# Rotary embedding on one core: the rotated half summed by VectorE instead of TensorE, tables loaded over 128 partitions

## The chip, the cores and the metric

The kernel runs on one core of a Trainium2 chip. Its time is device microseconds (us) of that core, from start to end of the program. A core has TensorE (PE in the profile; matmuls, which write to PSUM), VectorE (DVE), ScalarE (ACT), GpSimd (POOL) and SyncE (SP), and 16 DMA engines that move data between HBM and SBUF. [...] SP, ACT and POOL can start DMAs.

## The reference

```
x: (16, 512, 1024) float32 -> (16, 512, 16 heads, 64)
cos, sin: (512, 32) float32, one row for each position
x1, x2 = x[..., :32], x[..., 32:]
out[..., :32] = x1 * cos - x2 * sin
out[..., 32:] = x1 * sin + x2 * cos
```

33.55 MB are read and 33.55 MB written. The two tables are 64 KB each.

## The kernel before

The 16 batches are taken two at a time: 8 slabs of 4 MB. A slab is a tile of 128 partitions x 8192 float32; a partition holds 8 consecutive rows (positions) of 1024 elements, so partitions 0 to 63 hold one batch and 64 to 127 the other. Five slab buffers exist (`slots = 5`). Results are written back into the slab that the input came in, so a buffer is free for the next load only when its store has landed.

At the start SP issues the first five loads (L69-70). ACT's queue issues the loads of `cos` and `sin` (L77), each over 64 partitions with 1 KB rows. POOL builds an identity `ident` and a two-fold copy of it, `spread`. VectorE turns the tables into bf16 rows `cc1` (cos, cos) and `ss1` (sin, -sin); TensorE copies them to all 128 partitions with `spread` (L104), and VectorE writes them out as `cc` and `ss` (L106).

Then each slab is worked off in 4 passes of 2 rows (2048 elements in a partition):

1. ScalarE casts the piece to bf16: `xb` (L115).
2. VectorE makes two products, `t1 = xb * cc` (L120) and `t2 = xb * ss` (L121), all bf16.
3. TensorE adds them in PSUM: for each 512-wide bank a matmul of `ident` with `t1` (L125) and one of `ident` with `t2` read with its 32-wide halves exchanged (L127), 8 matmuls in a pass.
4. ScalarE copies the sum from PSUM back into the slab as float32 (L132).

After the fourth pass ACT's queue issues the slab's store (L133), and SP issues the load of slab s+5 (L135, L66), which waits for that store to land. A framework orders each engine's instructions and puts in the semaphores. In the order that it made, ScalarE's cast of the next slab's first piece stands ahead of the write-backs of the last pieces of the slab before; a cast that waits for its load therefore holds up the write-backs and the store behind it. Intermediate tiles have 3 buffers each, the PSUM sum has 2.

Of the kernel before, what the change touches and what calls it, by code (L numbers as in the profile page):

```python
# [2 lines left out]

# [4 lines left out]


@with_exitstack  # L10
def kernel(
    ctx: ExitStack,
    tc: tile.TileContext,
    x: bass.AP,
    cos: bass.AP,
    sin: bass.AP,
    num_heads: int,
    out: bass.AP,
):
    nc = tc.nc  # L20
    P = nc.NUM_PARTITIONS

    batch, seq, dim = x.shape
    nh = num_heads
    hd = dim // nh
    half = hd // 2
    bf16 = mybir.dt.bfloat16
    f32 = mybir.dt.float32

    nb = 2  # L30
    slots = 5
    lead = 5
    nslabs = batch // nb
    rpp = nb * seq // P
    W = rpp * dim
    SP = seq // rpp
    rows = 2
    PW = rows * dim
    BANK = 512
    hpb = BANK // hd  # L40

    out_flat = out.rearrange("b s h d -> b s (h d)")

    singles = ctx.enter_context(tc.tile_pool(name="singles", bufs=1))
    slabs = ctx.enter_context(tc.tile_pool(name="slabs", bufs=slots))
    tpool = ctx.enter_context(tc.tile_pool(name="tpool", bufs=3))
    psum = ctx.enter_context(tc.tile_pool(
        name="psum", bufs=2, space=bass.MemoryType.PSUM))


    def dram(t, s):
        return bass.AP(tensor=t.tensor, offset=t.offset + s * nb * seq * dim,
                       ap=[[W, P], [1, W]])


    def view(t, offset, *dims):
        return dataclasses.replace(t, offset=t.offset + offset,
                                   ap=[t.ap[0], *[list(d) for d in dims]])


    slab = {}


    def load(s):
        slab[s] = slabs.tile([P, W], f32, tag="slab", name="slab")
        nc.sync.dma_start(out=slab[s], in_=dram(x, s))  # L66


    for s in range(lead):  # L69
        load(s)  # L70

    cos_sb = singles.tile([SP, rpp * half], f32, tag="cos_sb")
    sin_sb = singles.tile([SP, rpp * half], f32, tag="sin_sb")
    for t, src in ((cos_sb, cos), (sin_sb, sin)):
        nc.scalar.dma_start(out=t, in_=bass.AP(  # L77
            tensor=src.tensor, offset=src.offset,
            ap=[[rpp * half, SP], [1, rpp * half]]))

    ident = singles.tile([P, P], bf16, tag="ident")
    masks.make_identity(nc, ident)
    spread = singles.tile([SP, P], bf16, tag="spread")
    for g in range(P // SP):
        nc.gpsimd.tensor_copy(out=spread[:, g * SP:(g + 1) * SP],  # L85
                              in_=ident[:SP, :SP])


    cc1 = singles.tile([SP, rpp * hd], bf16, tag="cc1")
    ss1 = singles.tile([SP, rpp * hd], bf16, tag="ss1")  # L90
    nc.vector.tensor_copy(  # L91
        out=cc1, in_=view(cos_sb, 0, (half, rpp), (0, 2), (1, half)))
    sin_rows = view(sin_sb, 0, (half, rpp), (1, half))
    nc.vector.tensor_copy(  # L94
        out=view(ss1, 0, (hd, rpp), (1, half)), in_=sin_rows)
    nc.vector.tensor_scalar_mul(  # L96
        out=view(ss1, half, (hd, rpp), (1, half)), in0=sin_rows, scalar1=-1.0)
    cc = singles.tile([P, rpp * hd], bf16, tag="cc")
    ss = singles.tile([P, rpp * hd], bf16, tag="ss")
    for wide, one in ((cc, cc1), (ss, ss1)):  # L100
        acc = psum.tile([P, PW], f32, tag="acc", name="acc")
        for q in range(0, rpp * hd, BANK):
            n = min(BANK, rpp * hd - q)
            nc.tensor.matmul(view(acc, q, (1, n)), spread, view(one, q, (1, n)),  # L104
                             start=True, stop=True)
        nc.vector.tensor_copy(out=wide, in_=view(acc, 0, (1, rpp * hd)))  # L106

    for s in range(nslabs):
        xs = slab.pop(s)
        for k in range(rpp // rows):  # L110
            xk = view(xs, k * PW, (1, PW))
            xb = tpool.tile([P, PW], bf16, tag="xb")
            t1 = tpool.tile([P, PW], bf16, tag="t1")
            t2 = tpool.tile([P, PW], bf16, tag="t2")
            nc.scalar.copy(out=xb, in_=xk)  # L115

            def tab(t):
                return view(t, k * rows * hd, (hd, rows), (0, nh), (1, hd))

            nc.vector.tensor_mul(out=t1, in0=xb, in1=tab(cc))  # L120
            nc.vector.tensor_mul(out=t2, in0=xb, in1=tab(ss))  # L121
            acc = psum.tile([P, PW], f32, tag="acc")
            for q in range(0, PW, BANK):
                bank = view(acc, q, (1, BANK))
                nc.tensor.matmul(bank, ident, view(t1, q, (1, BANK)),  # L125
                                 start=True, stop=False)
                nc.tensor.matmul(  # L127
                    bank, ident,
                    view(t2, q + half, (hd, hpb), (-half, 2), (1, half)),
                    start=False, stop=True)  # L130

            nc.scalar.copy(out=xk, in_=acc)  # L132
        nc.scalar.dma_start(out=dram(out_flat, s), in_=xs)  # L133
        if s + lead < nslabs:
            load(s + lead)  # L135


# [1 line left out]
_INS = ['x', 'cos', 'sin', 'num_heads']  # L139
_OUTS = [((16, 512, 16, 64), 'float32')]  # L140

_NUMBERS = {'num_heads': 16}


# [26 lines left out]
```

## Time and profile before

| | |
|---|---|
| time, median of 7 runs | 163.75 us (163.36 to 165.43) |
| time of the profiled execution | 163.58 us |
| its span in the profile | 161.8 us |
| busy: TensorE, VectorE, ScalarE | 78.2, 76.4, 117.3 us |
| granted TensorE clock, mean | 0.845 |

Every DMA of a slab, from the trace (issue time, plus time from issue to landing; us from the start of the span):

| slab | load issued | load landed | store issued | store landed |
|---|---|---|---|---|
| 0 | 0.7 | 13.7 | 34.7 | 57.6 |
| 1 | 1.2 | 23.7 | 53.8 | 78.1 |
| 2 | 1.6 | 33.4 | 68.6 | 97.5 |
| 3 | 2.1 | 48.0 | 84.1 | 116.8 |
| 4 | 2.8 | 68.5 | 98.8 | 131.5 |
| 5 | 57.7 | 87.8 | 114.5 | 141.1 |
| 6 | 78.2 | 107.2 | 134.4 | 150.9 |
| 7 | 97.5 | 126.7 | 149.7 | 160.8 |

The loads run on SP's queue and the stores on ACT's. "Landed" is when the semaphore of the transfer was complete. Where transfers of both queues are in flight, they share the same 16 DMA engines.

### The profile page before, as it was taken

The page shows a single profiled execution, that of the slowest core. Times are in us where ns is not written, and L with a number is a line of the kernel's source. Part 1 is how long each engine was busy: PE and PEld are TensorE (multiplying, and loading weights), DVE is VectorE, ACT ScalarE, POOL GpSimd, SP SyncE. Part 2 cuts the span into 40 slices and gives each one's busy share as a digit, 9 for nine tenths or more (in the row PEclk, how much of TensorE's full clock was granted, in tenths as well). Part 3 has the DMA queues.
Part 4 walks back from the last instruction along what each step waited for, and adds up shares of the span by engine and source line. Part 5 has one row for each costly group of instructions (what it writes and reads, how often), then busy time and mean ns, then how long its engine had stood idle before and what let it go on. Part 6 is the DMA issues. An engine that isn't in the chain of part 4 may idle for free.

```text
span 161.8 us, 811 instructions
## 1 busy us (share of the span) xinstructions
PE 78.2 (48%) x253; PEld 28.8 (18%) x258; DVE 76.4 (47%) x69; ACT 117.3 (72%) x65; POOL 1.1 (1%) x8
## 2 busy tenths in 40 slices
PE   0001179636059754942995388079754078084000
PEld 0000024212013221310332133023221022021000
DVE  0001699055099439806955484199335172280000
ACT  3006746994999999899989998979990697918000
POOL 2000000000000000000000000000000000000000
PEclk9999999999857998696599968957999957659855
DMA  7999999999999999999999999999999999996996
GB/s 243 413 397 405 405 478 413 405 478 413 397 478 421 397 494 401 405 486 405 407 478 405 415 470 413 413 470 413 421 470 401 421 470 405 421 470 300 389 389 259
DMA packets 2468, 67.29 MB, mean 416 GB/s; under 512 B 288, under 2 KB 416, under 8 KB 416
## 3 DMA queue, kind: packets, MB, share of 16 engines
q1 hardware_dynamic: 1152, 33.55, 48.8%
q10 hardware_dynamic: 1312, 33.69, 48.4%
q8 instruction: 2, 0.03, 0.1%
q14 instruction: 2, 0.02, 0.0%
HBM read 33.69 MB, written 33.55 MB: 416 GB/s over the span
## 4 chain that ended last, share of the span: by engine, by line
DMA 46%; PE 16%; ACT 14%; issue 9%; DVE 6%; ACTq 0%; DVEq 0%; SPq 0%
DMA slab<-in_x_dram 18%; DMA out_dram<-slab 18%; DMA sin_sb<-in_sin_dram 10%; PE acc L127 9%; ACT slab L132 8%; PE acc L125 7%; ACT xb L115 6%; DVE t L121 5%; DVE t L120 1%; PE acc L104 0%; ACTq L77 0%; DVE ss L94 0%; DVE ss L96 0%; DVEq L120 0%; ACTq L132 0%
## 5 line engine op out<-in xcount | busy, mean ns | idle before, releaser
L125 PE MATMUL acc<-t,ident 128*128 128x512 bf16 x123 | 56.4, 459 | 43.9 <-DVE t L120 33.3
L115 ACT CAST xb<-slab 128x2048 bf16<-128x2048 f32 x32 | 59.6, 1905 | 19.3 <-DMA slab<-in_x_dram 16.7
L132 ACT COPY slab<-acc 128x2048 f32<-128x2048 f32 x32 | 59.2, 1869 | 11.1 <-PE acc L127 10.6
L120 DVE TENSOR_TENSOR t<-xb,cc 128x2048 bf16<-128x2048 bf16 x32 | 39.1, 1222 | 51.4 <-ACT xb L115 51.4
L127 PE MATMUL acc<-t,ident 128*128 128x512 bf16 x128 | 57.6, 450 | 7.9 <-DVE t L121 7.3
L121 DVE TENSOR_TENSOR t<-xb,ss 128x2048 bf16<-128x2048 bf16 x32 | 39.0, 1218 | 0.0
L127 PEld LDWEIGHTS <-ident 128*128 128x128 bf16 x128 | 14.4, 112 | 58.6 <-issue 50.3
L125 PEld LDWEIGHTS <-ident 128*128 128x128 bf16 x128 | 14.2, 111 | 47.1 <-issue 28.7
L104 PE MATMUL acc<-cc,spread 64*128 64x512 bf16 x1 | 0.6, 582 | 12.8 <-DVE cc L91 12.8
L91 DVE CAST cc<-cos_sb 64x512 bf16<-64x512 f32 x1 | 0.4, 418 | 12.3 <-DMA cos_sb<-in_cos_dram 12.3
L104 PE MATMUL acc<-ss,spread 64*128 64x512 bf16 x1 | 0.6, 583 | 4.8 <-DVE ss L96 4.8
L115 ACT ACT_TABLE_LOAD x1 | 1.3, 1283 | 2.0 <-issue 2.0
L94 DVE CAST ss<-sin_sb 64x256 bf16<-64x256 f32 x1 | 0.3, 286 | 4.9 <-DMA sin_sb<-in_sin_dram 4.9
L104 PEld LDWEIGHTS <-spread 64*128 64x128 bf16 x2 | 0.2, 100 | 12.7 <-issue 10.9
L106 DVE CAST ss<-acc 128x512 bf16<-128x512 f32 x1 | 0.7, 691 | 0.1
L106 DVE CAST cc<-acc 128x512 bf16<-128x512 f32 x1 | 0.7, 676 | 0.0
L85 POOL COPY spread<-ident 64x64 bf16<-64x64 bf16 x2 | 0.4, 229 | 0.1
masks.py:199 POOL TENSOR_SCALAR_AFFINE_SELECT ident<-ident 128x128 bf16<-128x128 bf16 x1 | 0.3, 292 | 0.1
L96 DVE TENSOR_SCALAR ss<-sin_sb 64x256 bf16<-64x256 f32 x1 | 0.3, 278 | 0.0
masks.py:197 POOL MEMSET ident<- 128x128 bf16 x1 | 0.2, 204 | 0.3 <-POOLq L152 0.3
L152 POOL MEMSET const-bfloat16-1.0<- 128x1 bf16 x1 | 0.1, 102 | 0.0
L152 POOL MEMSET const-uint8-127<- 128x1 uint8 x1 | 0.1, 102 | 0.0
(2 smaller groups left out, 0.2 us busy)
## 6 DMA issues: line engine op xcount, KB each, us to landing
slab<-in_x_dram SPq DMA_DIRECT2D x8, 4096.0 KB, 29.6
out_dram<-slab ACTq DMA_DIRECT2D x8, 4096.0 KB, 25.5
cos_sb<-in_cos_dram ACTq DMA_DIRECT2D x1, 64.0 KB, 11.6
sin_sb<-in_sin_dram ACTq DMA_DIRECT2D x1, 64.0 KB, 16.3
```

The costliest lines, as they stand in the source:

```text
L85: nc.gpsimd.tensor_copy(out=spread[:, g * SP:(g + 1) * SP], in_=ident[:SP, :SP])
L91: nc.vector.tensor_copy(out=cc1, in_=view(cos_sb, 0, (half, rpp), (0, 2), (1, half)))
L94: nc.vector.tensor_copy(out=view(ss1, 0, (hd, rpp), (1, half)), in_=sin_rows)
L96: nc.vector.tensor_scalar_mul(out=view(ss1, half, (hd, rpp), (1, half)), in0=sin_rows, scalar1=-1.0)
L104: nc.tensor.matmul(view(acc, q, (1, n)), spread, view(one, q, (1, n)), start=True, stop=True)
L106: nc.vector.tensor_copy(out=wide, in_=view(acc, 0, (1, rpp * hd)))
L115: nc.scalar.copy(out=xb, in_=xk)
L120: nc.vector.tensor_mul(out=t1, in0=xb, in1=tab(cc))
L121: nc.vector.tensor_mul(out=t2, in0=xb, in1=tab(ss))
L125: nc.tensor.matmul(bank, ident, view(t1, q, (1, BANK)), start=True, stop=False)
L127: nc.tensor.matmul(bank, ident, view(t2, q + half, (hd, hpb), (-half, 2), (1, half)), start=False, stop=True)
L132: nc.scalar.copy(out=xk, in_=acc)
```

## The change

TensorE no longer takes part in the passes. A pass is 4 rows (4096 elements in a partition), so a slab has 2 passes and the kernel 16. In each, VectorE makes `t2 = xb * (sin, -sin)`, then `xb = xb * (cos, cos)` in place, then adds `t2`, read with its halves exchanged, to `xb`, in bf16 and in place. ScalarE casts in and, now from SBUF and from bf16, back into the slab. `t2` has one buffer, `xb` three. The cast of the next pass is written ahead of the write-back of this one, by hand.

The tables are loaded over 128 partitions with 512-byte rows by two DMAs on POOL's queue, issued beside the first slab's load. POOL builds `pick`, with which four small matmuls spread the rows; VectorE writes one table tile `tab` from PSUM with three instructions. In all it has 52 VectorE instructions where there were 69.

```diff
-    rows = 2
+    rows = 4
     PW = rows * dim
-    BANK = 512
-    hpb = BANK // hd
+    TW = rpp * half
...
     tpool = ctx.enter_context(tc.tile_pool(name="tpool", bufs=3))
+    t2pool = ctx.enter_context(tc.tile_pool(name="t2pool", bufs=1))
...
-    for s in range(lead):
+    load(0)
+    TR = seq // P
+    G = rpp // TR
+    raw = singles.tile([P, 2 * TR * half], f32, tag="raw")
+    for i, src in enumerate((cos, sin)):
+        nc.gpsimd.dma_start(out=view(raw, i * TR * half, (1, TR * half)), in_=bass.AP(
+            tensor=src.tensor, offset=src.offset,
+            ap=[[TR * half, P], [1, TR * half]]))
+    for s in range(1, slots):
         load(s)
...
-    for t, src in ((cos_sb, cos), (sin_sb, sin)):
-        nc.scalar.dma_start(out=t, in_=bass.AP(
-            tensor=src.tensor, offset=src.offset,
-            ap=[[rpp * half, SP], [1, rpp * half]]))
...
+    tab1 = singles.tile([P, 2 * TR * half], bf16, tag="tab1")
+    nc.vector.tensor_copy(out=tab1, in_=raw)
+    acc = psum.tile([P, 2 * TW], f32, tag="acc")
+    for i in range(2):
+        for g in range(G):
+            nc.tensor.matmul(view(acc, i * TW + g * TR * half, (1, TR * half)),
+                             view(pick, g * P, (1, P)),
+                             view(tab1, i * TR * half, (1, TR * half)),
+                             start=True, stop=True)
+    tab = singles.tile([P, 2 * rpp * hd], bf16, tag="tab")
...
+    def cast(u):
+        s, k = u
+        xb[u] = tpool.tile([P, PW], bf16, tag="xb", name="xb")
+        nc.scalar.copy(out=xb[u], in_=view(slab[s], k * PW, (1, PW)))
+    passes = [(s, k) for s in range(nslabs) for k in range(rpp // rows)]
+    cast(passes[0])
+    for i, u in enumerate(passes):
+        if i + 1 < len(passes):
+            cast(passes[i + 1])
+        s, k = u
+        xs, xu = slab[s], xb.pop(u)
+        t2 = t2pool.tile([P, PW], bf16, tag="t2")
+        for t, a in ((t2, rpp * hd), (xu, 0)):
+            nc.vector.tensor_mul(
+                out=t, in0=xu,
+                in1=view(tab, a + k * rows * hd, (hd, rows), (0, nh), (1, hd)))
+        nc.vector.tensor_add(
+            out=xu, in0=xu,
+            in1=view(t2, half, (hd, rows * nh), (-half, 2), (1, half)))
+        nc.scalar.copy(out=view(xs, k * PW, (1, PW)), in_=xu)
+        if k == rpp // rows - 1:
+            nc.scalar.dma_start(out=dram(out_flat, s), in_=xs)
+            if s + slots < nslabs:
+                load(s + slots)
-            nc.scalar.copy(out=xb, in_=xk)
-            nc.vector.tensor_mul(out=t1, in0=xb, in1=tab(cc))
-            nc.vector.tensor_mul(out=t2, in0=xb, in1=tab(ss))
-            acc = psum.tile([P, PW], f32, tag="acc")
-            for q in range(0, PW, BANK):
-                bank = view(acc, q, (1, BANK))
-                nc.tensor.matmul(bank, ident, view(t1, q, (1, BANK)),
-                                 start=True, stop=False)
-                nc.tensor.matmul(
-                    bank, ident,
-                    view(t2, q + half, (hd, hpb), (-half, 2), (1, half)),
-                    start=False, stop=True)
-            nc.scalar.copy(out=xk, in_=acc)
-        nc.scalar.dma_start(out=dram(out_flat, s), in_=xs)
-        if s + lead < nslabs:
-            load(s + lead)
```

More of the change, by code (lines that the diff above doesn't have):

```diff
@@ L31 @@
     slots = 5
-    lead = 5
     nslabs = batch // nb
@@ L46, with dram @@
     tpool = ctx.enter_context(tc.tile_pool(name="tpool", bufs=3))
+    t2pool = ctx.enter_context(tc.tile_pool(name="t2pool", bufs=1))
     psum = ctx.enter_context(tc.tile_pool(
[L48 to L53, printed above, removed]
+        name="psum", bufs=1, space=bass.MemoryType.PSUM))
+    def dram(t, s, a=0, n=W):
+        return bass.AP(tensor=t.tensor, offset=t.offset + s * nb * seq * dim + a,
+                       ap=[[W, P], [1, n]])
     def view(t, offset, *dims):
@@ L66, in load @@
         nc.sync.dma_start(out=slab[s], in_=dram(x, s))
-    for s in range(lead):
-        load(s)
-    cos_sb = singles.tile([SP, rpp * half], f32, tag="cos_sb")
-    sin_sb = singles.tile([SP, rpp * half], f32, tag="sin_sb")
-    for t, src in ((cos_sb, cos), (sin_sb, sin)):
-        nc.scalar.dma_start(out=t, in_=bass.AP(
-            tensor=src.tensor, offset=src.offset,
-            ap=[[rpp * half, SP], [1, rpp * half]]))
-    ident = singles.tile([P, P], bf16, tag="ident")
-    masks.make_identity(nc, ident)
@@ L83 @@
[L83 to L95, printed above, removed]
@@ L96 @@
-    nc.vector.tensor_scalar_mul(
[L97 to L118, printed above, removed]
-            nc.vector.tensor_mul(out=t1, in0=xb, in1=tab(cc))
-            nc.vector.tensor_mul(out=t2, in0=xb, in1=tab(ss))
-            acc = psum.tile([P, PW], f32, tag="acc")
-            for q in range(0, PW, BANK):
-                bank = view(acc, q, (1, BANK))
-                nc.tensor.matmul(bank, ident, view(t1, q, (1, BANK)),
-                                 start=True, stop=False)
-                nc.tensor.matmul(
-                    bank, ident,
-                    view(t2, q + half, (hd, hpb), (-half, 2), (1, half)),
-                    start=False, stop=True)
-            nc.scalar.copy(out=xk, in_=acc)
-        nc.scalar.dma_start(out=dram(out_flat, s), in_=xs)
-        if s + lead < nslabs:
-            load(s + lead)
+    load(0)
@@ new lines @@
+    TR = seq // P
[6 more added lines that the diff above has]
+    for s in range(1, slots):
+        load(s)
+    pick = singles.tile([P, G * P], bf16, tag="pick")
+    nc.gpsimd.memset(pick, 0.0)
+    for g in range(G):
+        part = view(pick, g * P, (SP, P // SP), (1, SP))
+        nc.gpsimd.affine_select(
+            out=part, in_=part, compare_op=mybir.AluOpType.not_equal, fill=1.0,
+            base=-g, pattern=[[0, P // SP], [-G, SP]], channel_multiplier=1)
@@ new lines @@
+    tab1 = singles.tile([P, 2 * TR * half], bf16, tag="tab1")
+    nc.vector.tensor_copy(out=tab1, in_=raw)
+    acc = psum.tile([P, 2 * TW], f32, tag="acc")
+    for i in range(2):
+        for g in range(G):
+            nc.tensor.matmul(view(acc, i * TW + g * TR * half, (1, TR * half)),
[3 more added lines that the diff above has]
+    tab = singles.tile([P, 2 * rpp * hd], bf16, tag="tab")
@@ new lines @@
+    nc.vector.tensor_copy(out=view(tab, 0, (hd, 2 * rpp), (1, half)),
+                          in_=view(acc, 0, (half, 2 * rpp), (1, half)))
+    nc.vector.tensor_copy(out=view(tab, half, (hd, rpp), (1, half)),
+                          in_=view(acc, 0, (half, rpp), (1, half)))
+    nc.vector.tensor_scalar_mul(
+        out=view(tab, rpp * hd + half, (hd, rpp), (1, half)),
+        in0=view(acc, TW, (half, rpp), (1, half)), scalar1=-1.0)
+    xb = {}
+    def cast(u):
+        s, k = u
+        xb[u] = tpool.tile([P, PW], bf16, tag="xb", name="xb")
+        nc.scalar.copy(out=xb[u], in_=view(slab[s], k * PW, (1, PW)))
```

## The prediction

> **What bounds the kernel now.** I read the page's slices and queues first, to see whether an engine or the DMAs fill the span:
>
> ```profile
> span 161.8 us, 811 instructions
> PE 78.2 (48%) x253; PEld 28.8 (18%) x258; DVE 76.4 (47%) x69; ACT 117.3 (72%) x65; POOL 1.1 (1%) x8
> DMA  7999999999999999999999999999999999996996
> DMA packets 2468, 67.29 MB, mean 416 GB/s; under 512 B 288, under 2 KB 416, under 8 KB 416
> q1 hardware_dynamic: 1152, 33.55, 48.8%
> q10 hardware_dynamic: 1312, 33.69, 48.4%
> ```
>
> No engine is full (ScalarE 72%), but the two queues together hold the 16 DMA engines for 97.2% of the span, and every slice except the first and a few at the end shows a 9. A chain of waits that changes hands between engines means little under such a row: what counts is when the DMA engines have nothing to do. Of 161.8 us they lack 2.8%, 4.5 us. Second, the stretches where that can be, as windows (the last three columns: clock, DMA share, GB/s):
>
> ```profile
> 2.00:12.00 10.00, 0.00 (x0) 0.00 (x0) 0.00 (x0) 1.24 (x1) 0.00 (x0) 1.00 0.96 396
> 12.00:22.00 10.00, 1.94 (x4) 0.41 (x4) 4.71 (x8) 5.66 (x4) 0.00 (x0) 1.00 1.01 423
> 142.00:152.00 10.00, 5.07 (x15) 1.70 (x14) 3.10 (x3) 3.87 (x3) 0.00 (x0) 0.81 0.89 383
> ...
> 147.00:148.00 1.00, 0.68 (x3) 0.10 (x1) 0.00 (x0) 1.00 (x2) 0.00 (x0) 1.00 1.14 492
> 148.00:149.00 1.00, 0.00 (x0) 0.00 (x0) 0.00 (x0) 1.00 (x1) 0.00 (x0) 1.00 0.23 98
> 149.00:150.00 1.00, 0.00 (x0) 0.00 (x0) 0.00 (x0) 0.68 (x1) 0.00 (x0) 1.00 0.15 66
> 150.00:151.00 1.00, 0.00 (x0) 0.00 (x0) 0.00 (x0) 0.00 (x0) 0.00 (x0) 1.00 1.22 524
> ```
>
> There is a thin start and a hole of about a microsecond ahead of 150. Third, what ScalarE did there (start, duration, engine, line):
>
> ```profile
> 126.76 1.90 ACT L115 CAST xb<-slab 128x2048 bf16<-128x2048 f32 x1 [5.12 <-DMA slab<-in_x_dram]
> ...
> 134.36 0.34 ACTq L133 DMA_DIRECT2D out_dram<-slab  x1
> 136.77 1.86 ACT L132 COPY slab<-acc 128x2048 f32<-128x2048 f32 x1 [0.57 <-PE acc L127]
> 138.53 3.70 ACT L115 CAST xb<-slab 128x2048 bf16<-128x2048 f32 x2
> 146.04 3.63 ACT L132 COPY slab<-acc 128x2048 f32<-128x2048 f32 x2 [3.81 <-PE acc L127]
> 149.70 0.34 ACTq L133 DMA_DIRECT2D out_dram<-slab  x1
> ```
>
> The last load lands at 126.7; the work on it issues the last store at 149.7, 23.0 us later, just as the store ahead of it runs out. But that hole is not all loss. Stores 4, 5 and 6 landed at 131.5, 141.1 and 150.9, 9.6 and 9.8 us apart, and the last one at 160.8, only 9.9 later. Most engines were idle for a microsecond, the slowest for some 0.2 us (9.9 less the mean of 9.7), and the slowest sets the landing.
>
> [...] a transfer takes 9.7 us alone (load 1 to 2) and 19.4 while the other queue is full (load 6 to 7: 107.2 to 126.7). [...] no POOL DMA is in this trace. [...] the trace has 1222 and 1218 ns (L120, L121). [...]
>
> **The passes.** Removed: 256 matmuls and their weight loads, 32 casts, 32 write-backs, 64 products. Added: 16 casts, 16 write-backs, 48 VectorE instructions, all 4096 wide.
>
> - ScalarE, cast: [...] The write-back reads bf16 from SBUF instead of PSUM; the nearest rows are the cast from SBUF (1905 ns) and the PSUM copy (1869 ns)[...], I take 3.61. Back to back they overlap by 0.1 (three casts took 5.50, not 5.72), so 2 x 3.51 = 7.0 a pass.
> - VectorE: [...] The compiled order lets each wait for the one before it (in-place product, sum, single `t2`). The trace has no such pair: products that don't wait start 0.09 before the last ends; a matmul after its product starts 0.04 to 0.05 after it; the one ScalarE instruction put down to the ScalarE one before it was 0.34 late. So between -0.09 and +0.34, I take 0.06: 3 x 2.35 = 7.05 a pass (6.6 to 7.9).
>
> Casts run a pass ahead, so ScalarE and VectorE overlap, and a pass costs about 7.1 us, a slab 14.2. In the shared stretch a slab takes the DMA engines 19.4 us. So both engines will wait for loads in the second half, as ScalarE does now.
>
> The start: load 0 lands at 13.7, cast to 17.3, VectorE 17.4 to 24.4 and to 31.5, write-back to 35.1, store 0 issued at 35.1 (34.7 before). Store 1 follows at 49.3. Loads alone keep the engines busy to about 52 and store 0 to 61, so store 1 has over 10 us in hand. Load 5 waits for store 0, load 7 for store 2, and these are paced by the engines: the last load again lands at about 126.7.
>
> The end, by the compiled order: cast (7,0) 126.8 to 130.4, write-back (6,1) to 133.9 and with it store 6 (134.4 before), cast (7,1) to 137.4; VectorE 130.4 to 137.5 and to 144.5; write-back (7,1) 144.6 to 148.2; last store at 148.2, 1.5 us earlier. Store 6 runs to about 149.2 on most engines and later on the slowest, so the last one is in line in time, and the hole closes. That is worth the 0.2 us above, 0.8 at most by the windows' mean (142 to 152 lacks 11%, of which 0.3 lies beyond one store's change-over). With 0.34 between VectorE's instructions the store is issued at 149.9 and nothing is won, 0.2 lost.
>
> **The tables.** Same bytes, 64 KB twice, but 256 rows of 512 B for 128 of 1 KB, on POOL's queue. Load 0 took 13.0 us from issue to landing, the last store, alone, 11.1; the 2 to 12 window is 27 GB/s under the next, 0.6 us. So the tables and the cold start cost 0.6 to 1.9 us now. If POOL's packets take 8 rows each, there are fewer turns between queues and up to 0.9 is won; if each row is a turn, 16 rows an engine for 8, up to 0.9 is lost. I take 0.2 won, for the packing. When they land matters less: before, `sin` came at 17.6. With 0.4 for the cast (64x512: 418 ns), four matmuls under 0.6 each and PSUM copies of 0.69 and twice about 0.4, `tab` is there 3.5 to 4.3 us after the rows. Rows by 13 hide fully behind load 0 and its cast. Up to 24 they delay store 0, but not beyond the slack. POOL's `pick` is ready long before, by its memset and select of 0.2 and 0.3 us.
>
> Sum, against the profiled execution: 163.58 - 0.2 - 0.2 = 163.2, span 161.4. That execution lay 0.17 under the median, so 163.3.
>
> **Rivals.** *The start gets cheaper* (0.25): the rows come in two packets, and load 0 lands 0.8 to 1.2 earlier; everything shifts with it, as the DMA engines are never out of work: 163.3 - 1.0 = 162.3. For it: 13.0 against 11.1. Against: the table's bytes alone are 0.3 us, and a cold start may be the rest.
>
> *VectorE becomes the bound* (0.09, slower): the sum reads `t2` in runs of 32 with a backward step. [...] It decides from 8.0 us a pass on, where 17.4 + 16 x 8.0 + 3.7 reaches 149.2; in the tail alone from 7.6. [...]
>
> *The tables come late* (0.11, slower): every row and semaphore takes a turn between 32 KB packets. Before, sin's five turns took 5.3 us; 18 turns end near 12.3 + 13 x 1.06 = 26[...]; `tab` at 30.4, store 0 at 48.2, store 1 at 62.3. The engines run out at 61.1: 1.6 us of hole, with dearer turns 2 us: 165.2.
>
> The forecast itself, DMA-bound and near unchanged, has 0.55; its own range is 162.7 to 164.2.
>
> **How the numbers follow.** A change of under 0.5% (0.8 us: 162.93 to 164.57) can't be told from none here. Faster: most of the first rival and a little of the forecast, 0.29. Slower: 0.09 + 0.10, and 0.02 of dearer turns, 0.21. Same: 0.50. The range 162.2 to 165.3 leaves out VectorE's bound and the edges.
>
> **What would show it.** VectorE groups at 2.29 us for both operations, and 2.35 between starts; ScalarE at 3.61. Store 0 at 35, last store before its forerunner's end, no low slice near the end. DMA share 97 to 98%. Load 0 landing at 13.7 or less: each tenth earlier is a tenth of the time. I am wrong if the loads' cadence of 19.4 changes, for then the DMA engines are not what I take them for; if load 0 lands over a microsecond later or earlier; or if POOL's queue adds time outside the loop, which nothing here shows.

## The result and the profile after

The changed kernel takes 162.77 us (median of 15 runs, 162.43 to 163.21) against 163.50 (36 runs). The ratio is 0.9954, with a 95% interval of 0.9937 to 0.9971: about 0.75 us faster (0.5 to 1.0), just inside the 0.5% that the prediction counts as no change. The profiled execution took 162.60, with a span of 160.7 us. Here and below a time is the median of all executions, while a ratio leaves out executions over 1.5% slower than the fastest of their kernel, which are two of six in before_tables_pool and one of 22 in pool_no_hole.

First the page of the changed kernel: span, engines, the row of DMA slices, packets and queues (packets, MB, share of 16 engines).

```profile
span 160.7 us, 197 instructions
PE 0.6 (0%) x4; PEld 0.4 (0%) x4; DVE 111.7 (69%) x52; ACT 114.8 (71%) x33; POOL 2.3 (1%) x9
DMA  7999999999999999999999999999999999999993
...
DMA packets 2369, 67.25 MB, mean 418 GB/s; under 512 B 288, under 2 KB 288, under 8 KB 320
...
q1 hardware_dynamic: 1152, 33.55, 49.3%
q10 hardware_dynamic: 1152, 33.55, 48.3%
q0 software_dynamic: 64, 0.13, 0.2%
q14 instruction: 1, 0.01, 0.0%
```

TensorE is gone and VectorE has its work, 111.7 us for 76.4, but the DMA row is what it was: full. Only the low slices near the end have moved into the last one. In q0 the 256 table rows are 32 packets of 4 KB and 32 semaphore packets (64 in all; 32 is also the difference between "under 8 KB" and "under 2 KB"). So POOL's queue did gather 8 rows into a packet: by count one for each DMA engine and table, two for each engine in all. In the prediction this is an assumption, as the trace of the kernel before has no POOL DMA. The packets start in two groups of 16, within 5.9 to 6.6 and 8.5 to 9.2, each beside 15 packets of the loads. The last line comes up again further down.

Next the groups of the same page (busy us and mean ns of one, then the idle time ahead of them):

```profile
L117 ACT CAST xb<-slab 128x4096 bf16<-128x4096 f32 x16 | 57.5, 3601 | 24.8 <-DMA slab<-in_x_dram 24.8
L137 ACT CAST slab<-xb 128x4096 f32<-128x4096 bf16 x16 | 57.7, 3604 | 7.2 <-DVE xb L133 7.1
L130 DVE TENSOR_TENSOR t<-xb,tab 128x4096 bf16<-128x4096 bf16 x16 | 36.7, 2292 | 19.3 <-ACT xb L117 18.4
L133 DVE TENSOR_TENSOR xb<-xb,t 128x4096 bf16<-128x4096 bf16 x16 | 36.7, 2292 | 0.5
```

The sum with exchanged halves (L133) takes the same 2.292 us as a product, so reading `t2` in runs of 32 with a backward step did not slow it. ScalarE waits 24.8 us for loads.

Last the end, as the windows of the changed kernel (the last columns are clock, DMA share, GB/s) and then as its timeline:

```profile
147.00:148.00 1.00, 0.00 (x0) 0.00 (x0) 0.00 (x0) 0.41 (x1) 0.00 (x0) 1.00 1.21 524
148.00:149.00 1.00, 0.00 (x0) 0.00 (x0) 0.00 (x0) 0.00 (x0) 0.00 (x0) 1.00 0.53 229
149.00:150.00 1.00, 0.00 (x0) 0.00 (x0) 0.00 (x0) 0.00 (x0) 0.00 (x0) 1.00 0.76 328
150.00:151.00 1.00, 0.00 (x0) 0.00 (x0) 0.00 (x0) 0.00 (x0) 0.00 (x0) 1.00 1.21 524
```

```profile
126.09 3.60 ACT L117 CAST xb<-slab 128x4096 bf16<-128x4096 f32 x1 [5.96 <-DMA slab<-in_x_dram]
...
133.23 0.34 ACTq L139 DMA_DIRECT2D out_dram<-slab  x1
...
143.80 3.60 ACT L137 CAST slab<-xb 128x4096 f32<-128x4096 bf16 x1 [3.50 <-DVE xb L133]
147.44 0.34 ACTq L139 DMA_DIRECT2D out_dram<-slab  x1
```

The last load is there at 126.1, the last store is issued 21.3 us later (23.0 before), and the shares around 149 are 0.53 and 0.76 where they were 0.23 and 0.15. It lands at 159.9, 12.4 after its issue and 9.7 after the store ahead of it, as one that stood in line. Everything else is a fraction earlier as well: load 2 landed at 32.8 (33.4 before), store 6 at 150.2 (150.8).

That leaves two accounts. In the first, the tables on POOL's queue make a shorter start, and the passes close the hole. In the second the queue of the tables is of no matter, and all comes from the passes.

### The profile page after: what moved, and what is told of

The parts are those of the page before. It is cut to its first block, busy times and chain, and to the rows that moved or that the text cites. A ratio compares the mean times of both kernels' runs of the same rounds, so it can differ in the third digit from the quotient of the medians.

```text
span 160.7 us, 197 instructions
## 1 busy us (share of the span) xinstructions
PE 0.6 (0%) x4; PEld 0.4 (0%) x4; DVE 111.7 (69%) x52; ACT 114.8 (71%) x33; POOL 2.3 (1%) x9
## 3 DMA queue, kind: packets, MB, share of 16 engines
q1 hardware_dynamic: 1152, 33.55, 49.3%
q10 hardware_dynamic: 1152, 33.55, 48.3%
HBM read 33.69 MB, written 33.55 MB: 418 GB/s over the span
## 4 chain that ended last, share of the span: by engine, by line
DMA 47%; ACT 22%; DVE 21%; issue 0%; ACTq 0%; SPq 0%; DVEq 0%
DMA slab<-in_x_dram 26%; DMA out_dram<-slab 21%; ACT slab L137 11%; ACT xb L117 11%; DVE xb L133 7%; DVE t L130 7%; DVE xb L130 7%; ACTq L137 0%; SPq L65 0%; DVEq L130 0%
## 5 line engine op out<-in xcount | busy, mean ns | idle before, releaser
L117 ACT CAST xb<-slab 128x4096 bf16<-128x4096 f32 x16 | 57.5, 3601 | 24.8 <-DMA slab<-in_x_dram 24.8
L137 ACT CAST slab<-xb 128x4096 f32<-128x4096 bf16 x16 | 57.7, 3604 | 7.2 <-DVE xb L133 7.1
L130 DVE TENSOR_TENSOR t<-xb,tab 128x4096 bf16<-128x4096 bf16 x16 | 36.7, 2292 | 19.3 <-ACT xb L117 18.4
L133 DVE TENSOR_TENSOR xb<-xb,t 128x4096 bf16<-128x4096 bf16 x16 | 36.7, 2292 | 0.5
L130 DVE TENSOR_TENSOR xb<-xb,tab 128x4096 bf16<-128x4096 bf16 x16 | 36.7, 2292 | 0.5
L102 DVE CAST tab<-acc 128x512 bf16<-128x512 f32 x1 | 0.7, 693 | 0.7 <-PE acc L96 0.7
L75 POOL DMA_DIRECT2D raw<-in_cos_dram x1 | 0.7, 674 | 0.8 <-POOLq L158 0.8
L96 PE MATMUL acc<-tab,pick 128*128 128x128 bf16 x4 | 0.6, 300 | 11.4 <-DVE tab L92 11.4
L87 POOL TENSOR_SCALAR_AFFINE_SELECT pick<-pick 128x128 bf16<-128x128 bf16 x2 | 0.5, 288 | 0.1
L75 POOL DMA_DIRECT2D raw<-in_sin_dram x1 | 0.5, 534 | 0.0
```

The lines of the kernel that those rows point to most:

```text
L75: nc.gpsimd.dma_start(out=view(raw, i * TR * half, (1, TR * half)), in_=bass.AP(tensor=src.tensor, offset=src.offset, ap=[[TR * half, P], ...
L87: nc.gpsimd.affine_select(out=part, in_=part, compare_op=mybir.AluOpType.not_equal, fill=1.0, base=-g, pattern=[[0, P // SP], [-G, SP]], c ...
L96: nc.tensor.matmul(view(acc, i * TW + g * TR * half, (1, TR * half)), view(pick, g * P, (1, P)), view(tab1, i * TR * half, (1, TR * half)) ...
L102: nc.vector.tensor_copy(out=view(tab, 0, (hd, 2 * rpp), (1, half)), in_=view(acc, 0, (half, 2 * rpp), (1, half)))
L117: nc.scalar.copy(out=xb[u], in_=view(slab[s], k * PW, (1, PW)))
L130: nc.vector.tensor_mul(out=t, in0=xu, in1=view(tab, a + k * rows * hd, (hd, rows), (0, nh), (1, hd)))
```

## The experiments

Each ratio is against the kernel before, run beside it on the same chip. The medians of the kernel before differ a little between these groups (163.50 to 163.76), so kernels of different groups are best compared by their ratios. Landings are of one profiled execution each.

**Tables on ACT's queue.** One line of the changed kernel:

```diff
-        nc.gpsimd.dma_start(out=view(raw, i * TR * half, (1, TR * half)), in_=bass.AP(
+        nc.scalar.dma_start(out=view(raw, i * TR * half, (1, TR * half)), in_=bass.AP(
```

> The changed kernel with only the issuing queue of the two table loads put back: ACT's queue instead of POOL's, still 256 rows of 512 B. Theory (packing): on ACT's queue every row is a packet of its own, 16 a DMA engine and two semaphores, so the tables cost load 0 and load 1 more than before the change; sin lands near 26, load 1 lands 24 or later instead of 23.1, and the time is 0.6 to 1.5 us over the changed kernel's 162.77: 163.4 to 164.3, with the last store still issued before its forerunner has ended. Rival (the queue is of no matter, the gain lies in the passes): 162.6 to 162.9.

162.51 us, ratio 0.9938 (0.9916 to 0.9961). The theory fails: the time is not over the changed kernel's but, if anything, a little under the rival's. The packets are as the theory had them: the sin table landed at 23.4 instead of 10.9, and the queue shows every row apart:

```profile
q1 hardware_dynamic: 1152, 33.55, 49.3%
q10 hardware_dynamic: 1440, 33.69, 48.6%
DMA packets 2593, 67.25 MB, mean 418 GB/s; under 512 B 288, under 2 KB 544, under 8 KB 544
```

q10 has 288 packets more than the 1152 of the changed kernel: 256 rows and 32 semaphores. But load 1 landed at 23.2, against 23.1 in the changed kernel, so the small packets delayed no load noticeably. Store 0 was issued at 43.6 instead of 34.7, and that cost nothing either: loads were in flight until 57.7.

**The other halves of the change.** The kernel before with its tables on POOL's queue, and the changed passes with the old tables:

```diff
 # before_tables_pool: kernel before
-        nc.scalar.dma_start(out=t, in_=bass.AP(
+        nc.gpsimd.dma_start(out=t, in_=bass.AP(
 # passes_alone: the changed kernel, with lines 74-106 of the kernel before
+    tab = singles.tile([P, 2 * rpp * hd], bf16, tag="tab")
+    cc = view(tab, 0, (1, rpp * hd))
+    ss = view(tab, rpp * hd, (1, rpp * hd))
```

> The kernel before with only the issuing queue of its two table loads changed to POOL's: 64 partitions, rows of 1 KB, TensorE sums as before. Theory: 4 rows of 1 KB make one packet for each engine, the start gets as short as with the change, load 1 lands near 23.1, and 0.5 to 0.7 us of 163.50 go: 162.8 to 163.0; the hole ahead of the last store stays. Rival (the gain lies in the passes): 163.4 to 163.6.

> The changed passes (no TensorE sums, 4096 wide) with the tables of the kernel before: loaded on ACT's queue over 64 partitions and spread as there. Theory: only the hole at the end closes, worth 0.2 to 0.3 us: 163.2 to 163.3, load 1 landing at 23.7 as before. Rival (the gain lies in the passes): 162.7 to 162.9.

The changed passes alone took 162.67 us, ratio 0.9951 (0.9928 to 0.9975), as in the rival: the whole gain, with sin landing at 17.5 and load 1 at 23.5. The tables on POOL's queue in the kernel before did not help by 0.5 us: they made it slower, by a ratio of 1.0201 (1.0155 to 1.0246), 3.3 us, which neither forecast had. Its six executions lie far apart, 166.19 to 171.31 with a median of 167.47, and the trace is of one that took 169.78, so it shows the effect larger than it mostly is. Its first store, its timeline at the end, and its windows:

```profile
31.04 0.38 ACTq L133 DMA_DIRECT2D out_dram<-slab  x1
...
132.36 1.90 ACT L115 CAST xb<-slab 128x2048 bf16<-128x2048 f32 x1 [5.16 <-DMA slab<-in_x_dram]
...
139.95 0.34 ACTq L133 DMA_DIRECT2D out_dram<-slab  x1
...
156.00 0.34 ACTq L133 DMA_DIRECT2D out_dram<-slab  x1
```

```profile
145.00:150.00 5.00, 1.62 (x4) 0.51 (x4) 3.44 (x4) 3.32 (x2) 0.00 (x0) 0.55 0.97 419
150.00:155.00 5.00, 3.96 (x12) 1.35 (x11) 1.19 (x2) 2.76 (x2) 0.00 (x0) 0.77 0.08 33
155.00:160.00 5.00, 0.00 (x0) 0.00 (x0) 0.00 (x0) 0.97 (x1) 0.00 (x0) 0.92 0.74 315
```

The hole is some 5 us long in this execution (share 0.08). The last load lands at 132.3 instead of 126.7, and the last store is issued 23.7 after it, nearly as before (23.0). Why is the last load late? With the tables early, VectorE begins at 15.7 instead of 19.4, and the first store is issued at 31.0 instead of 34.7. From there on stores share the DMA engines with the loads (in the trace of the kernel before, between 100 and 105, they hold 50.0% and the loads 48.5%), and loads 3, 4 and all after them are late (51.3 for 48.0, 72.5 for 68.5). That is a reading; two runs further down test it.

**No table loads.** VectorE fills the table with ones; the rotation is left out.

> The changed kernel without the two table loads: VectorE fills the table with ones, so the rotation is left out of the computation. It shows what the table loads still cost. Theory (with the packing they are nearly free): load 0 lands 0.2 to 0.4 us earlier than 13.4 and the time is 162.4 to 162.6. Rival (the tables still hold up the start): load 0 lands at 11.9 to 12.2, as early after its issue as the last store, and the time is 161.4 to 161.8.

162.17 us, ratio 0.9911 (0.9883 to 0.9938). Load 0 landed at 13.0, so the rival's 11.9 to 12.2 is out; the time is below the theory's range. Against tables_on_act and passes_alone, both with the tables on ACT's queue, the tables cost 0.3 to 0.5 us; against the changed kernel, on POOL's, the ratios give 0.4%, 0.7 us. The intervals overlap, so the size is rough. An estimate from the record, 0.13 MB at the 418 GB/s of the span, gives 0.3 us for the bytes alone.

**VectorE made slower.** One more product in each pass, N = 1024 or 2048 wide:

```diff
+        extra = t2pool.tile([P, N], bf16, tag="extra")
+        nc.vector.tensor_mul(out=extra, in0=view(xu, 0, (1, N)), in1=view(t2, 0, (1, N)))
         nc.vector.tensor_add(
```

> The changed kernel with one more VectorE product in each pass, 1024 wide, into a tile that nothing reads, ahead of the sum: 0.69 us and 0.04, so a pass goes from 7.05 to 7.78 on VectorE, 11.7 us in all. Theory (the DMA engines are the bound and VectorE has up to 7.6 to 8.0 us a pass): the last store is issued at 126.1 + 3.6 + 15.6 + 3.7 = 149.0 instead of 147.4, and the time grows by 0 to 0.4 us: 162.8 to 163.2. Rival (VectorE's work sets the time): 5 to 12 us more.

> The same with the extra product 2048 wide: 1.22 us and 0.04, a pass takes 8.31. Theory: past the bound; VectorE runs without a gap from 17.0, its last pass ends at 150.0, the last store is issued at 153.7 and lands 11.1 later at 164.8, 5.0 after the changed kernel's 159.8: 167.3 to 168.2. Rival (the DMA engines hide this too): under 163.5.

The wider one took 167.82, ratio 1.0248 (1.0220 to 1.0275), as computed: VectorE had no gap to speak of, the store was issued at 154.0 (153.7 forecast) and landed at 165.1 (164.8). The narrower one took 163.73, ratio 1.0005 (0.9984 to 1.0025): by the ratios 0.5% or 0.8 us over the changed kernel instead of at most 0.4, though 11.7 us of work were added. In its trace, which is of the slowest of its 14 executions (164.55), the last load came at 126.9, the last store was issued at 149.7, not 149.0, and landed at 161.9.

**The last store made later.** The end of the very last write-back, done twice, N = 2048 or 4096 wide:

```diff
+        if i == len(passes) - 1:
+            nc.scalar.copy(out=view(xs, k * PW, (1, N)), in_=view(xu, 0, (1, N)))
         if k == rpp // rows - 1:
```

> The changed kernel with half of the very last write-back done twice, so that only the last store is later, by 1.8 us: issued at 149.2, where the kernel before had it at 149.7. Theory (the hole ahead of the last store is worth 0.2 to 0.3 us): 163.0 to 163.1. Rival (a store that is issued before its forerunner has landed loses nothing): 162.7 to 162.8.

> The same with the whole last write-back done twice, 3.5 us: the last store is issued at 150.9, after its forerunner has landed at 150.2. Theory: from here on the delay counts in full, landing at 150.9 + 11.1 = 162.0, 2.2 us over the changed kernel: 164.8 to 165.2. Rival (the end is bound by the DMA engines whatever the issue): under 163.5.

162.95 (0.9955, 0.9939 to 0.9971), between the two forecasts, and 164.40 (1.0049, 1.0029 to 1.0068), a little under the theory. The stores, one line of each timeline:

```profile
148.73 0.34 ACTq L141 DMA_DIRECT2D out_dram<-slab  x1
```

```profile
150.52 0.34 ACTq L141 DMA_DIRECT2D out_dram<-slab  x1
```

They were issued somewhat earlier than forecast (149.2 and 150.9). The first landed at 159.9, exactly where the changed kernel's lands with its store at 147.4, and by ratio nothing was lost. The second landed at 161.6, 11.1 after its issue. So in these two traces and the changed kernel's the last landing is the later of 159.9 and issue plus 11.1, and they meet near 148.7. The trace of vector_plus_1024 does not fit the rule: issued at 149.7, its last store landed at 161.9, 12.2 later.

By this rule nearly the whole gain would be the hole, since the kernel before had its store at 149.7 and its landing at 160.8. The next run tests that from the other side.

**The kernel before without the hole, twice.** The last two passes of the last slab are left out:

```diff
-        for k in range(rpp // rows):
+        for k in range(rpp // rows if s < nslabs - 1 else 2):
```

> The kernel before, with the last two of the four passes of the last slab left out (4 of its 8 rows in a partition go back as they came), so that the last store is issued early, near 139 instead of 149.7, while all bytes are still moved. Theory (the time is the later of the DMA engines' own end, landing near 159.8, and the last store's issue plus 11.1, and the whole gain of the change is the hole ahead of the last store): landing at 159.8 to 160.0, 162.5 to 162.8. Rival (the hole costs only 0.2 to 0.3 us, as the spacing of the landings suggested, and the rest lies in the start or the middle): 163.1 to 163.3.

> The kernel before with its table loads on POOL's queue (before_tables_pool, 167.47) and the last two passes of the last slab left out as in before_no_hole. Theory (its 4 us are nothing but a later last load and so a longer hole): the last load lands near 131 again, the last store is issued near 145, landing at 159.8 to 160.0: 162.5 to 162.8. Rival (POOL's queue slows the transfers themselves): over 164.5.

163.40 us, ratio 0.9979 (0.9962 to 0.9996). The store was issued at 139.2 and yet landed only at 160.9. Its DMA windows have no hole:

```profile
148.00:149.00 1.00, 0.00 (x0) 0.00 (x0) 0.00 (x0) 0.00 (x0) 0.00 (x0) 0.50 0.99 426
149.00:150.00 1.00, 0.00 (x0) 0.00 (x0) 0.00 (x0) 0.00 (x0) 0.00 (x0) 0.50 0.76 328
```

So the hole is worth 0.21% of the median (0.04 to 0.38), 0.34 us, and the theory that it is all falls: with the passes of the kernel before, the DMA engines' own end lies later.

The traces show more of this. A transfer's semaphore is counted up 16 times as it lands (the page has 288 packets under 512 B for 18 transfers), which I read as once for each DMA engine. For the last store the middle of these 16 counts lies at 159.0 to 159.1 in all five traces of before_no_hole, before_again (below), the changed kernel, passes_alone and tables_on_act. The last count, which is the landing, comes at 160.4 and 160.9 in the two with TensorE sums, and at 159.7 to 159.9 in the three without. Read so, most engines end together, and stragglers make the difference. The page of the kernel before has two lines that may bear on it:

```profile
q8 instruction: 2, 0.03, 0.1%
q14 instruction: 2, 0.02, 0.0%
```

These are four packets for the one of the changed kernel, which has 197 instructions instead of 811. In the trace of the kernel before they start at 62.9, 78.7, 89.6 and 123.6, and the two of q8 take over 1 us each. In the transfers that land after the first, second and third of them one, two and three counts come 0.9 us or more after the first count; after the fourth it is five. In passes_alone the only such packet starts at 119.9; until then all counts of a transfer lie within 0.3 us (load 3 on), and from the next landing to the end just one comes late, by about 1.0 us. No run changes these packets alone, and engines can lag without them (3.3 us at store 0 of vector_plus_2048), so this is a likely cause and not a shown one. It would also say why the hole cost so little: in it the stragglers caught up, and the last store's 16 counts lay within 0.2 us at 160.8, no later than the straggler of before_no_hole.

With the tables on POOL's queue the same two passes left out brought the ratio from 1.0201 down to 1.0054 (1.0029 to 1.0080), 164.88 us. Most of that loss was the hole, and about 0.5% was not. The theory's 162.5 to 162.8 fails, and the time is the rival's; the run after this one tests the rival's cause. By the middle counts the loads 4 to 7 came 19.6 to 20.0 us apart in the two kernels with early first stores, and 19.3 to 19.4 in the traces of the kernel before and of the changed kernel. Why is open.

**Tables on POOL's queue, first pass held back.** In before_tables_pool:

```diff
+    held = singles.tile([P, rpp * hd], bf16, tag="held")
+    for _ in range(19):
+        nc.vector.tensor_mul(out=held, in0=cc, in1=ss)
     for s in range(nslabs):
```

> before_tables_pool with 19 small VectorE products between the tables and the first pass, which hold that pass back from 15.7 to about 19.4, where it began in the kernel before. Theory (what made it slower is that the first store comes 3.7 us earlier and takes turns with the loads for longer, so that the last load lands later by as much or more): store 0 issued at 34.7, last load landed at 126 to 127, last store at 149 to 150: 163.3 to 163.7. Rival (POOL's queue, not the earlier store): 166 to 168.

163.27 us, ratio 0.9970 (0.9953 to 0.9987). Adding useless work to VectorE took 2.3% off by the ratios, 3.8 us. The first product of the first pass began at 20.5, the last load landed at 123.9 (forecast 126 to 127), and these are the first and the last store:

```profile
35.43 0.38 ACTq L137 DMA_DIRECT2D out_dram<-slab  x1
...
148.46 0.34 ACTq L137 DMA_DIRECT2D out_dram<-slab  x1
```

So POOL's queue by itself does not make the kernel slower; the earlier start of the passes, and of the stores with them, does. That its time is 0.3% under the kernel before fits a hole that is nearly closed.

**The kernel before once more.**

> The kernel before, unchanged, for a second trace: how far its landings repeat. Theory: last store issued at 149.5 to 149.9 and landed 11.1 later; load 1 landed anywhere between 23.1 and 23.7. Rival (the first trace was a fair account of the start): load 1 at 23.6 to 23.8 and store 6 at 150.8 to 151.0 again.

163.75 us, ratio 1.0005 (0.9983 to 1.0028). In this profiled execution (163.23) the hole was absent: the last load landed at 124.9, the last store was issued at 147.6 and landed at 160.4. The windows where the hole was:

```profile
148.00:149.00 1.00, 0.00 (x0) 0.00 (x0) 0.00 (x0) 0.00 (x0) 0.00 (x0) 1.00 0.76 328
149.00:150.00 1.00, 0.00 (x0) 0.00 (x0) 0.00 (x0) 0.00 (x0) 0.00 (x0) 1.00 0.84 360
```

So the first expectation fails: the hole was there in one trace of this kernel and not in the other, and the last load landed at 126.7 and at 124.9. The times of single executions (163.11 to 165.07) suggest that it comes and goes, and a median holds both kinds. The rival held about: load 1 at 23.9, just past its range, and store 6 at 150.8.

## Why the prediction was right, and where it was not

- *The DMA engines are the bound.* Right. 11.7 us more VectorE work cost 0.8 us, and loads 4 to 7 came 19.4 us apart in the changed kernel (by the middle counts), as before; its two queues held the DMA engines for 97.6% of the span.
- *A pass of 7.0 to 7.1 us.* Right: 3.60 for each ScalarE instruction, 2.29 for each VectorE one, starts 2.33 apart when one waits for the one before, so 0.04 between them, not 0.06. Last store at 147.4 for 148.2; its load was 0.6 earlier. The 3.61 and 2.29 in the prediction were the author's estimates: the trace of the kernel before shows the same operations at 2048 wide only, at 1905 and 1869 ns and at 1222 and 1218 ns.
- *The hole closes, worth 0.2, at most 0.8.* Right in place, and 0.34 us in size by before_no_hole (0.07 to 0.62). Reading the spacing of landings rather than the mean share of the windows gave the better figure. Unrounded, the spacing gives 0.3: the last four stores landed at 131.52, 141.17, 150.83 and 160.81.
- *The tables, 0.2 won by packing.* The step that failed. The packing took place, and sin came 6.7 us earlier, but tables_on_act and passes_alone reach the same time without it. The intervals are too wide to exclude a gain of 0.2 us; none was seen. What failed with it is "each tenth earlier is a tenth of the time". By its middle count, load 2 was half a microsecond earlier with the tables over 128 partitions, on POOL's queue or on ACT's (32.5), than in passes_alone with the old tables (33.0), yet all three ended together, at 159.0 to 159.1 by the middle counts. A head start at load 2 was lost on the way; how is open.
- *What stands in its place.* Some 0.25% lies between before_no_hole (0.9979) and the changed passes (0.9938 to 0.9955), at the edge of what the intervals can tell. In the traces it is the stragglers among the 16 counts: the last landing at 159.7 to 159.9 in the changed passes, with any tables, and at 160.4 and 160.9 with TensorE sums, the tables on ACT's queue and no hole. The prediction has nothing of this. The passes were changed as a whole (width, sum, order of casts), and no run takes them apart, so the cause stays open; the instruction packets are the candidate that the traces offer.
- *The start rival, 0.25.* Its signs were partly there (load 0 at 13.3 for 13.7, load 1 at 23.1), but passes_alone did as well with load 1 at 23.5.
- *VectorE as the bound.* Not at 7.05 us a pass; at 8.3 it was one, as vector_plus_2048 showed with 167.82. The point in the tail, 7.6, fits: at 7.8 the time was 0.8 us longer. That the sum might run slower than a product was only the author's assumption; both took 2.292 us.
- *Late tables.* Harmless at 23.4, as the prediction's slack up to 24 says. The turns that it counts are in the trace of the kernel before: cos goes in four groups of 16 rows, within 5.9 to 6.7, 7.2 to 8.0, 8.4 to 9.2 and 9.8 to 10.6, each beside 15 or 16 packets of the loads. Of sin, 32 rows go within 12.4 to 13.2 and 16 each within 13.8 to 14.6 and 15.1 to 15.9, then its semaphores within 16.5 to 17.2. So these turns start some 1.3 us apart, not 1.06, and sin's 5.3 us were four of them, not five. What it did not see is the other side: tables that come too early can hurt, as before_tables_pool did.

In sum 0.4 us were forecast and some 0.75 measured, so the time was met within 0.6 us. In part that is luck: of the two terms of 0.2 one held and came out a little larger, the other was not found, and a gain that the prediction does not name made up for it.

## What to carry to other kernels

When the DMA engines are full, compare each last store's issue with the landing of the store ahead of it: up to a point (148.7 here) its lateness was free, and 1.8 us beyond it cost 1.45. Look at the slowest of the 16 counts of a landing and not only at mean shares: that is where the traces have the remainder of this gain (160.4 and 160.9 against 159.7 to 159.9). Work that begins earlier is not always a gain: with the first store at 31.0 instead of 34.7 the last load landed at 132.3 instead of 126.7, and the 23.7 us of serial work behind it were then exposed. To find which half of a change pays, run each half alone: here the tables, whose story was plain, paid nothing that could be measured.

## What was not expected of the hardware

- Small packets on ACT's queue between the loads' 32 KB packets (33.55 MB in 1024 packets) delayed themselves, not the loads: with 256 rows apart, by count 16 for each DMA engine, sin landed at 23.4 instead of 10.9, with load 1 at 23.2 and 23.1.
- Holding the first pass back from 15.7 to 20.5, and the first store from 31.0 to 35.4, made a kernel 2.3% faster (ratio 1.0201 to 0.9970).
- With stores from 31.0 on, a pair of load and store took 19.6 to 20.0 us; in the traces of the kernel before and of the changed kernel, with stores from 34.7 or later, 19.3 to 19.4.
- The middle of the 16 counts of the last landing came at the same time with TensorE sums and without (159.0 to 159.1); only the last count did not (160.4 and 160.9 against 159.7 to 159.9).
